# Join factors of the first dilated pair sent through DRAM instead of repeated and turned on chip

## The chip, the cores and the metric

The kernel runs on one core of a Trainium2 chip. The metric is the device time of one execution in microseconds (us); it is given as the median of three runs. The core has five engines that run side by side and meet by semaphores: TensorE (matmuls and transposes), VectorE, ScalarE, GpSimd and SyncE. SyncE's queue issues nearly all transfers of this kernel; 16 DMA engines carry them out. In the profile TensorE is called PE (its weight loads PEld), VectorE DVE, ScalarE ACT, GpSimd POOL and SyncE SP.

## The reference

A decoder trunk of two layers on 1024 tokens of width 1024, in float32. Each layer does

```python
h = rmsnorm(x, norm1[l])
qa, ka, va, qb, kb, vb, gate_pre = split(h @ w_in[l])
o_a = dilated_mixture(qa, ka, va)           # 12 heads of 64, three groups of 4
o_b = stick_breaking_attention(qb, kb, vb)  # 4 heads of 64
merged = g_a * (o_a @ w_br[l, :256]) + g_b * (o_b @ w_br[l, 256:])
x = x + merged @ w_o[l]
x = x + ffn(rmsnorm(x, norm2[l]))
```

The dilated mixture has three groups with dilation 1, 4 and 16. Each group gives an output `o` and a log-sum `lse` for each token and head, and the groups are mixed by

```python
alpha = softmax(stack(lses), axis=0)
o = sum(alpha[..., None] * stack(outs), axis=0)
```

So for every token and head there is one factor per group. A factor multiplies all 64 channels of its head at that token. This document is about how the factors get from where they are computed to where they multiply.

## The kernel before

**Layout.** Activations lie with channels on the 128 partitions and tokens along the free axis. The four mixture heads go in two pairs: pair 0 is heads 0 and 1, pair 1 heads 2 and 3. A pair's output fills 128 partitions: 64 channels of head 0 of the pair, then 64 of head 1. Group 1 (dilation 1) is computed by `near_item`, into the tile `on`. Groups 2 and 3 (dilation 4 and 16) are computed together by `far_item`, into the tile `ot`: eight items per pair (two heads, four residues `r` of the token modulo 4), named T00 to T07 for pair 0 and T10 to T17 for pair 1. So the mixture becomes a join of two parts, near and far.

**One far item.** `score` (L892) makes scores on TensorE (L646, L647, tile `z`), takes the row minimum of the negated scores on VectorE (L916) and the exponential with its row sum on ScalarE (L917, tile `p1`). `turn` (L921) transposes the result on TensorE (L924 to L926) into a PSUM bank with tag `t`, and splits it in a high and a low part (`parts`, L649): a cast on ScalarE (L141, `p1h`) and a subtraction on VectorE (L148, `p1l`). `apply` (L929) multiplies by the values (L934, L936). The last of these folds the result into `ot` (L661, L662) and, after the last item of a pair, calls `join`.

**Statistics and factors.** Minimum and sum of the far pass lie with tokens on partitions (tile `st1`). Those of the near pass come by way of DRAM (`dn`, `near_stats`, L948) in the same layout. `factors` (L952), called at the end of the score of the pair's last item, computes two factors (near and far) for each of 2 heads x 8 blocks of 128 tokens, in ten small instructions: tile `f`, 128 tokens x 2 x 16. A join needs them with channels on partitions, each repeated 64 times. So four ScalarE copies (L974) repeat each factor along the free axis into two tiles `fx` (tag `p4`, four buffers that the far items' `p1` also use), and `half_of` in `join` (L977) transposes them: eight 128x128 TensorE transposes (L988) per half of the tokens, into two PSUM banks, one with tag `t` and one with tag `o`. Then VectorE multiplies and adds in three instructions per half (L991 to L993), reading the factors from PSUM.

**Dense work and its order.** While the attention items run, projections of the layer run in between them, cut in shares of six 128x512 matmuls (class `Dense`, L222; L1017 to L1019). `attend` (L369) walks through the items and calls `dense.advance` between their steps; for far items it adds 0.58 of a share per step. `dense.at(n, f)` calls `f` when `n` more shares have been issued. `join` places its halves at 2 and at 4 (`JOIN`) shares. The order on TensorE is exactly the program's (a manual schedule). On the other engines a planner orders the instructions at build time, by priority (program order, or 200 ahead with `high_priority(offset=AHEAD)`) and by when it believes their inputs are ready; the order is then fixed, and each engine works through its queue in turn, waiting where an input is not there. `LAST["dve"]` holds the last split of a turn; a dependency without a semaphore on it keeps an instruction behind that split in VectorE's queue.

**Who reads the join.** The joined `on` is read by `in_two("a")` in `mixer` (L1353) after all items, when it is split into `oh_a`, `ol_a` for the branch projections. The tile `ot` has one buffer, used by pair 0, then by pair 1. The second pair's join is the last work before the branch projections.

Of the kernel before, what the change touches and what calls it, by code (L numbers as in the profile page):

```python
# [7 lines left out]
F32 = mybir.dt.float32  # L8
# [4 lines left out]
ALU = mybir.AluOpType  # L13
# [3 lines left out]
P = 128  # L17
T = 1024
D = 1024
KD = D // P  # L20
HF = 512
# [12 lines left out]
PT = 6  # L34
# [5 lines left out]
NO_SYNC = mybir.DependencyInfo(mybir.DependencyClass.NoSync, mybir.DependencyReason.DATA)  # L40
# [11 lines left out]
X_AT = (3, 5, 7, 9)  # L52
AHEAD = 200
JOIN = 4


def f32(ap):
# [4 lines left out]
def trunk_kernel(ctx, tc, x, norm1, w_in, b_gate, w_br, w_o, norm2, w_up, conv_w, conv_b, w_down, norm_f, out, depth=None, probe=None):  # L62
    nc = tc.nc
    act, dve, pe, pool = nc.scalar, nc.vector, nc.tensor, nc.gpsimd
# [21 lines left out]
    LAST = {}  # L86
# [34 lines left out]
    sq = [dr.tile([2, 2, 64, T], F32, name=f"sq{i}") for i in range(4)]  # L121
    sv = [dr.tile([P, n, KD, P], F32, name=f"sv{n}") for n in (4, 2, 2)]
    dn = [dr.tile([4, T], F32, name=f"dn{i}") for i in range(2)]

    def bank(tag, name):
        return ps.tile([P, 512], F32, tag=tag, name=name)
# [434 lines left out]
    R = {}  # L561
# [83 lines left out]
    def scores(o, qt, ql, k):  # L645
        pe.matmul(o, qt, k, start=True, stop=False, skip_group_check=True)  # L646
        pe.matmul(o, ql, k, start=False, stop=True, skip_group_check=True)  # L647

    def parts(src, n, name):  # L649

        hi, lo = small(name + "h", F32R), small(name + "l", F32R)
        with tc.high_priority(offset=AHEAD):
            split(hi[:, :n], lo[:, :n], src[:, :n], "is")
        return hi, lo
# [228 lines left out]
    def far_item(dense, pr, s, r, share):  # L883
        i = 8 * pr + 4 * s + r
        slot = 2 * pr + s
        if s == 0 and r == 0:
            R["st1", pr] = sb.tile([P, 2, 2, 2, 4], F32, tag="st1", bufs=2, name="st1")
            R["ot", pr] = None
        st = R["st1", pr]
        shared = {}  # L890

        def score():  # L892
            if r == 0:
                bias = share["bias"] = sb.tile([P, 2, 256], F32, tag="bias", name="bias1")
                dve.tensor_scalar(bias[:, 0, :], base0, 4.0 * SLOPES[4 + slot], None, ALU.mult)
                dve.tensor_scalar(bias[:, 1, :], base2, 4.0 * SLOPES[8 + slot], None, ALU.mult)
            bias = share["bias"]
            pt = shared["p"] = sb.tile([P, T], F32, tag="p4", bufs=4, name="p1")
            z0, z1 = bank("s", "z10"), bank("s", "z11")
            t = R["kq", i % 2]  # L900
            for g in range(2):
                scores(z0[:, P * g : P * g + P], t[:, g, 1, 0:P], t[:, g, 2, 0:P], t[:, g, 0, 0:P])
            for g in range(2):
                scores(z1[:, 256 * g : 256 * g + 256], t[:, g, 1, P:256], t[:, g, 2, P:256], t[:, g, 0, :])
            dense.scored = i + 1
            if (s, r) == (1, 0):
                near_stats(pr)
            for n in range(2):
                flat = pt[:, 256:768] if n else pt[:, 0:256]
                if n:  # L910
                    zz, pp, bb = z1, flat, bias.rearrange("p g c -> p (g c)")
                else:
                    zz, pp, bb = z0[:, 0:256].rearrange("p (g c) -> p g c", g=2), flat.rearrange("p (g c) -> p g c", g=2), bias[:, :, P:256]
                nm = st[:, 0, s, n, r : r + 1]
                with tc.high_priority(offset=AHEAD):
                    LAST["red"] = dve.tensor_tensor_reduce(pp, zz, bb, 1.0, 3e38, ALU.add, ALU.min, nm).ins.name  # L916
                    act.activation(flat, flat, AF.Exp, bias=nm, scale=-1.0, accum_out=st[:, 1, s, n, r : r + 1])  # L917
            if (s, r) == (1, 3):
                factors(pr)

        def turn(g):  # L921
            pt = shared["p"]
            tp = bank("t", "t1")
            pe.transpose(tp[:, 0:P], pt[:, P * g : P * g + P], ident)  # L924
            pe.transpose(tp[:, P : 2 * P], pt[:, 256 + 256 * g : 384 + 256 * g], ident)
            pe.transpose(tp[:, 2 * P : 3 * P], pt[:, 384 + 256 * g : 512 + 256 * g], ident)  # L926
            shared[g] = parts(tp, 384, "p1")

        def apply(g):  # L929
            if r % 2 == 0 and g == 0:  # L930
                share["o"] = bank("o", "o1")
            o, oc, vt = share["o"], 256 * (r % 2), R["v", i][:, g]
            for p in (0, 1):
                pe.matmul(o[:, oc : oc + 256], vt[:, 0:P], shared[g][p][:, 0:256], start=(r % 2 == 0 and g == 0 and p == 0), stop=False, skip_group_check=True)  # L934
# [12 lines left out]

    def near_stats(pr):  # L948
        sn = R["sn", pr] = sb.tile([P, 2, 2, 2, 4], F32, tag="sn", bufs=1, name="sn")
        nc.sync.dma_start(sn.rearrange("j a s n r -> j (a s) n r"), tok_view(dn[pr]))  # L950

    def factors(pr):  # L952

        sn, st = R["sn", pr], R["st1", pr]
        nat, far_ = (t.rearrange("j a s n r -> j a (s n r)") for t in (sn, st))
        w = sb.tile([P, 6, 16], F32, tag="sw", bufs=1, name="sw")
        f = R["f", pr] = sb.tile([P, 2, 2, 2, 4], F32, tag="sf", bufs=1, name="sf")
        ff = f.rearrange("j a s n r -> j a (s n r)")
        dve.tensor_tensor(w[:, 0, :], nat[:, 0, :], far_[:, 0, :], ALU.min)
        dve.tensor_tensor(w[:, 1, :], w[:, 0, :], nat[:, 0, :], ALU.subtract)  # L960
        dve.tensor_tensor(w[:, 2, :], w[:, 0, :], far_[:, 0, :], ALU.subtract)
        act.activation(w[:, 1:3, :], w[:, 1:3, :], AF.Exp)
        dve.tensor_tensor(w[:, 3, :], w[:, 1, :], nat[:, 1, :], ALU.mult)
        dve.tensor_tensor(w[:, 4, :], w[:, 2, :], far_[:, 1, :], ALU.mult)
        dve.tensor_tensor(w[:, 3, :], w[:, 3, :], w[:, 4, :], ALU.add)
        dve.reciprocal(w[:, 5, :], w[:, 3, :])
        dve.tensor_tensor(ff[:, 0, :], w[:, 1, :], w[:, 5, :], ALU.mult)
        dve.tensor_tensor(ff[:, 1, :], w[:, 2, :], w[:, 5, :], ALU.mult)

        R["fx", pr] = []  # L970
        for a in range(2):
            fx = sb.tile([P, 2, 4, 2, 64], F32, tag="p4", bufs=4, name="fx")
            for s in range(2):
                act.copy(fx[:, :, :, s, :], f[:, a, s, :, :].unsqueeze(3).to_broadcast([P, 2, 4, 64]))  # L974
            R["fx", pr].append(fx.rearrange("p n r s c -> p n r (s c)"))

    def join(dense, pr):  # L977

        fx, on, ot = R["fx", pr], R["on"], R["ot", pr]
        mine = on[:, pr, :].rearrange("p (n j r) -> p n r j", n=2, r=4)  # L980
        other = ot.rearrange("p (r n j) -> p n r j", r=4, n=2)

        def half_of(n):
            spread = []
            for a in range(2):
                o = bank("to"[a], "j_ps")
                for r in range(4):
                    pe.transpose(o[:, r * P : (r + 1) * P], fx[a][:, n, r, :], ident)  # L988
                spread.append(o.rearrange("p (r j) -> p r j", r=4))
            t = small("jn").rearrange("p (r j) -> p r j", r=4)  # L990
            dve.tensor_tensor(t, other[:, n], spread[1], ALU.mult)  # L991
            dve.tensor_tensor(mine[:, n], mine[:, n], spread[0], ALU.mult)
            dve.tensor_tensor(mine[:, n], mine[:, n], t, ALU.add)  # L993

        dense.at(2, lambda: half_of(0))
        dense.at(JOIN, lambda: half_of(1))

# [1174 lines left out]
```

## Time and profile before

| | |
|---|---|
| median of three runs | 2615.91 us (2615.09 to 2616.14) |
| the profiled execution | 2618.04 us |
| its span, from first to last instruction | 2616.1 us |
| TensorE busy | 2606.0 us |
| VectorE busy | 2089.5 us |
| ScalarE busy | 1357.6 us |
| GpSimd busy | 102.2 us |
| DMA queue of SP | 465.90 MB, 55.3% of 16 engines |

Times in rows of the trace are microseconds from the start of the span. A row of a time list has the start, the duration, the engine, the line, the operation, output and inputs, and in brackets how long the engine stood idle before and what ended that. A row of the chain of waits has start, duration, engine, tile and line; "issue" in it is time that the profile ascribes to nothing. Groups give minimum, median and maximum of the duration in nanoseconds, or busy time and mean. The shown duration of a matmul is longer than the interval between two of them, since they are pipelined; the interval between starts is what one costs.

### The profile page before, as it was taken

To read this page: it belongs to the slowest core of one execution; us is meant where nothing else is said; L and a number is where in the kernel's file an instruction comes from. 1 tells how busy PE (TensorE), PEld (TensorE's weight loads), DVE (VectorE), ACT (ScalarE), POOL (GpSimd) and SP (SyncE) were. 2 spreads that over 40 slices of the span, in tenths; PEclk is the share of its full clock that TensorE was granted. 3 is DMA by queue.
4 is the path that set the end of the run, shared out by engine and by line. 5 is a ranking of instruction groups with operands and counts; after the bars stand their busy time and mean duration, and the time that the engine had idled before them with its cause. 6 is when DMAs were issued, how large, how long until landed. Compare 5 with 4: busy or idle time off the path is not lost.

```text
span 2616.1 us, 36210 instructions
## 1 busy us (share of the span) xinstructions
PE 2606.0 (100%) x12736; PEld 2185.2 (84%) x12736; DVE 2089.5 (80%) x3484; ACT 1357.6 (52%) x2533; POOL 102.2 (4%) x135
## 2 busy tenths in 40 slices
PE   9999999999999999999999999999999999999999
PEld 8888888888888888888888888888888888888888
DVE  7877777795988888897677788777869888889965
ACT  6555666574554555422445555666645555544225
POOL 3000000020000000000000000000300000000000
PEclk9999999999999999999999999999999999999999
DMA  7434578873344444688344436787633344447962
GB/s 254 151 120 132 161 207 217 214 247 93 93 145 153 145 164 142 234 326 317 145 145 147 125 128 180 203 231 210 207 99 119 125 161 146 150 164 260 347 238 111
DMA packets 400418, 468.22 MB, mean 179 GB/s; under 512 B 24308, under 2 KB 315500, under 8 KB 398444
## 3 DMA queue, kind: packets, MB, share of 16 engines
q1 hardware_dynamic: 400220, 465.90, 55.3%
q8 instruction: 101, 1.65, 0.3%
q14 instruction: 81, 0.66, 0.1%
q10 hardware_dynamic: 16, 0.00, 0.0%
HBM read 303.23 MB, written 162.59 MB: 178 GB/s over the span
## 4 chain that ended last, share of the span: by engine, by line
PE 96%; DVE 1%; DMA 1%; ACT 1%; issue 1%; SPq 0%; POOL 0%; DVEq 0%; ACTq 0%
PE u_a L1019 6%; PE u_a L1018 6%; PE u_a L1017 6%; PE d_ps L1780 5%; PE d_ps L1781 5%; PE d_ps L1782 5%; PE i_a L1017 5%; PE i_a L1019 5%; PE i_a L1018 5%; PE u_c L1017 3%; PE u_c L1019 3%; PE u_c L1018 3%; PE i_c L1017 3%; PE i_c L1019 3%; PE i_c L1018 3%; PE o_ps L183 2%
## 5 line engine op out<-in xcount | busy, mean ns | idle before, releaser
L141 ACT CAST w_hi<-up_a 128x512 fp32r<-128x512 f32 x280 | 173.9, 622 | 276.5 <-DVE up_a L1634 120.5
L148 DVE TENSOR_TENSOR w_lo<-up_a,w_hi 128x512 fp32r<-128x512 f32 x280 | 189.3, 688 | 83.6 <-ACT w_hi L141 83.6
L141 ACT CAST w_hi<-in_a 128x512 fp32r<-128x512 f32 x252 | 156.2, 622 | 162.9 <-PE i_c L1018 38.0
L148 DVE TENSOR_TENSOR w_lo<-in_a,w_hi 128x512 fp32r<-128x512 f32 x252 | 172.7, 687 | 75.8 <-ACT w_hi L141 67.0
L1788 DVE TENSOR_TENSOR x<-x,d_ps 128x512 f32<-128x512 f32 (+1 forms) x228 | 153.4, 674 | 65.0 <-PE d_ps L1782 61.6
L1780 PE MATMUL d_ps<-gd_in,w_hi 128*128 128x512 f32 (+1 forms) x340 | 130.0, 382 | 0.0
L1782 PE MATMUL d_ps<-gd_in,w_lo 128*128 128x512 f32 (+1 forms) x340 | 129.8, 382 | 0.0
L1781 PE MATMUL d_ps<-gd_in,w_hi 128*128 128x512 f32 (+1 forms) x340 | 129.7, 382 | 0.0
L1019 PE MATMUL u_a<-hh,w_lo 128*128 128x512 f32 x320 | 124.5, 389 | 0.0
L1018 PE MATMUL u_a<-hl,w_hi 128*128 128x512 f32 x320 | 124.5, 389 | 0.0
L1017 PE MATMUL u_a<-hh,w_hi 128*128 128x512 f32 x320 | 124.5, 389 | 0.0
L1017 PE MATMUL u_a<-t_hi,w_hi 128*128 128x512 f32 x320 | 124.5, 389 | 0.0
L1019 PE MATMUL u_a<-t_hi,w_lo 128*128 128x512 f32 x320 | 124.5, 389 | 0.0
L1018 PE MATMUL u_a<-t_lo,w_hi 128*128 128x512 f32 x320 | 124.5, 389 | 0.0
L1017 PE MATMUL i_a<-hh,w_hi 128*128 128x512 f32 x288 | 119.2, 414 | 0.0
L1017 PE MATMUL i_a<-t_hi,w_hi 128*128 128x512 f32 x288 | 118.3, 411 | 0.0
L1780 PE MATMUL d_ps<-gd_in,wd 128*128 128x512 f32 (+1 forms) x292 | 113.9, 390 | 0.0
L1019 PE MATMUL i_a<-hh,w_lo 128*128 128x512 f32 x288 | 113.2, 393 | 0.0
L1019 PE MATMUL i_a<-t_hi,w_lo 128*128 128x512 f32 x288 | 113.0, 393 | 0.0
L1018 PE MATMUL i_a<-t_lo,w_hi 128*128 128x512 f32 x288 | 112.9, 392 | 0.0
L1018 PE MATMUL i_a<-hl,w_hi 128*128 128x512 f32 x288 | 112.8, 392 | 0.0
L1782 PE MATMUL d_ps<-gd_in,wd 128*128 128x512 f32 (+1 forms) x292 | 112.8, 386 | 0.0
(380 smaller groups left out, 7834.9 us busy)
## 6 DMA issues: line engine op xcount, KB each, us to landing
gd<-g SPq DMA_DIRECT2D x154, 512.0 KB, 3.3
gd_in<-gd SPq DMA_DIRECT2D x154, 512.0 KB, 5.9
up_a<-in_w_up_dram SPq DMA_DIRECT2D x80, 512.0 KB, 5.2
in_a<-in_w_in_dram SPq DMA_DIRECT2D x72, 512.0 KB, 5.3
wd_raw<-in_w_down_dram SPq DMA_DIRECT2D x22, 1024.0 KB, 11.2
gin<-gs SPq DMA_DIRECT2D x32, 512.0 KB, 3.8
w_raw<-in_w_o_dram SPq DMA_DIRECT2D x64, 256.0 KB, 2.9
gs<-u SPq DMA_DIRECT2D x48, 256.0 KB, 3.2
```

The source lines that it names most:

```text
L141: one = act.copy(hi, src)
L148: two = dve.tensor_tensor(lo, src, f32(hi), ALU.subtract)
L183: pe.matmul(o, lh, rl, start=False, stop=False, skip_group_check=share)
L1017: pe.matmul(o, w[0][:, c], rh, start=(first and i == 0), stop=False, skip_group_check=True)
L1018: pe.matmul(o, w[0][:, c], rl, start=False, stop=False, skip_group_check=True)
L1019: pe.matmul(o, w[1][:, c], rh, start=False, stop=(last and i == 3), skip_group_check=True)
L1780: pe.matmul(o[:, sub], wh[:, c], gh[:, sub], start=(i == 0 and k in (0, 4, 5)), stop=False, skip_group_check=True)
L1781: pe.matmul(o[:, sub], wh[:, c], gl[:, sub], start=False, stop=False, skip_group_check=True)
L1782: pe.matmul(o[:, sub], wl[:, c], gh[:, sub], start=False, stop=(i == m - 1), skip_group_check=True)
L1788: dve.tensor_tensor(x, x, o[:, sub], ALU.add)
```

## The change

For the first pair only (`pr == 0`), in both layers:

- `factors` writes the far factors in the order in which the tile `ot` has its tokens (residue before half), in two small VectorE instructions instead of one. The four ScalarE copies are not made.
- Four dense shares later (`SEND`), the 32 rows of factors are transposed once on TensorE (a 128x32 tile to 32x128), copied to SBUF by ScalarE, and written to a new DRAM tile `fd` (4 rows of 1024 tokens) by a transfer issued from GpSimd. Four more GpSimd-issued transfers read each row back, repeated over 64 partitions, into two tiles `fx` of 128 x 1024 (the same tag and size as the old ones).
- The join's halves are placed 3 and 5 shares after `join` instead of 2 and 4. They have no transposes: VectorE multiplies `ot` in place by the far factors, `on` by the near ones, and adds. Both multiplications are kept behind the last split of a turn.

The second pair's factors and join are as they were.

```diff
 JOIN = 4
+SEND = 4
...
+    fd = dr.tile([4, T], F32, name="fd")
...
             if (s, r) == (1, 3):
-                factors(pr)
+                factors(dense, pr)
...
-    def factors(pr):
+    def factors(dense, pr):
...
         dve.tensor_tensor(ff[:, 0, :], w[:, 1, :], w[:, 5, :], ALU.mult)
-        dve.tensor_tensor(ff[:, 1, :], w[:, 2, :], w[:, 5, :], ALU.mult)
+        if pr:
+            dve.tensor_tensor(ff[:, 1, :], w[:, 2, :], w[:, 5, :], ALU.mult)
+        else:
+            one, two = (w[:, k, :].rearrange("j (s n r) -> j s n r", s=2, n=2) for k in (2, 5))
+            for x in range(2):
+                dve.tensor_tensor(fr[:, 16 + 8 * x : 24 + 8 * x].rearrange("j (r n) -> j n r", n=2), one[:, x], two[:, x], ALU.mult)
+
+        if pr == 0:
+            R["fx", pr] = [sb.tile([P, T], F32, tag="p4", bufs=4, name="fx") for _ in range(2)]
+
+        def send():
+            tp = bank("t", "f_t")
+            pe.transpose(tp[0:32, 0:P], fr, ident)
+            row = sb.tile([32, P], F32, tag="pt", bufs=PT, name="f_r")
+            with tc.high_priority(offset=AHEAD):
+                act.copy(row, tp[0:32, 0:P])
+            nc.gpsimd.dma_start(fd.rearrange("c (k p) -> (c k) p", p=P), row)
+            for a in range(2):
+                for x in range(2):
+                    nc.gpsimd.dma_start(R["fx", pr][a][64 * x : 64 * x + 64, :], fd[2 * a + x : 2 * a + x + 1, :].to_broadcast([64, T]))
+
+        if pr == 0:
+            dense.at(SEND, send)
+            return
...
     def join(dense, pr):
...
+        def half_sent(n):
+            first, second = R["fx", pr]
+            mine, far = on[:, pr, n * HF : (n + 1) * HF], ot.rearrange("p (r n j) -> p n r j", r=4, n=2)[:, n]
+            mine = mine.rearrange("p (j r) -> p r j", r=4)
+            one = dve.tensor_tensor(far, far, second.rearrange("p (r n j) -> p n r j", r=4, n=2)[:, n], ALU.mult)
+            two = dve.tensor_tensor(mine, mine, first[:, n * HF : (n + 1) * HF].rearrange("p (r j) -> p r j", r=4), ALU.mult)
+            dve.tensor_tensor(mine, mine, far, ALU.add)
+            for x in (one, two):
+                tc.add_manual_dep(x.ins, LAST["dve"], NO_SYNC, reason="in turn")
+
+        if pr == 0:
+            dense.at(JOIN - 1, lambda: half_sent(0))
+            dense.at(JOIN + 1, lambda: half_sent(1))
+            return
```

More of the change, by code (lines that the diff above doesn't have):

```diff
@@ L958, in factors @@
         ff = f.rearrange("j a s n r -> j a (s n r)")
+        fr = f.rearrange("j a s n r -> j (a s n r)")
         dve.tensor_tensor(w[:, 0, :], nat[:, 0, :], far_[:, 0, :], ALU.min)
@@ L977, in join @@
     def join(dense, pr):
-        fx, on, ot = R["fx", pr], R["on"], R["ot", pr]
+        on, ot = R["on"], R["ot", pr]
+        def half_sent(n):
[11 more added lines that the diff above has]
+            return
+        fx = R["fx", pr]
         mine = on[:, pr, :].rearrange("p (n j r) -> p n r j", n=2, r=4)
```

## The prediction

> **What bounds the kernel.** I read the page's first part, then the chain of waits, then the time order of the stretch in which the first pair is joined.
>
> ```profile
> span 2616.1 us, 36210 instructions
> PE 2606.0 (100%) x12736; PEld 2185.2 (84%) x12736; DVE 2089.5 (80%) x3484; ACT 1357.6 (52%) x2533; POOL 102.2 (4%) x135
> PE 96%; DVE 1%; DMA 1%; ACT 1%; issue 1%; SPq 0%; POOL 0%; DVEq 0%; ACTq 0%
> ```
>
> TensorE carries 96% of the chain that ends last. So an instruction taken from TensorE is worth its interval, if nothing else is then late, and work taken from ScalarE or VectorE is worth something only where TensorE waits for it. The chain near the first layer's first join shows both kinds:
>
> ```profile
> 470.78 0.57 ACT fx L974
> ...
> 471.82 1.13 ACT fx L974 x2
> 472.95 0.53 ACT w_hi L141
> 473.51 0.69 DVE w_lo L148
> 474.20 0.60 DVE p L916
> ...
> 475.66 0.37 ACT p1h L141
> ...
> 476.05 0.57 DVE p1l L148
> ...
> 476.67 0.39 PE o L934
> ...
> 485.33 0.87 PE j_ps L988 x8
> ...
> 490.70 0.87 PE j_ps L988 x8
> ```
>
> The four copies that repeat the factors (L974) hold ScalarE from 470.78 to 472.95, 2.17 us; a weight cast, a split and a softmax step queue behind them, and TensorE's matmul of L934 comes late at 476.67. The same chain stands in layer 1. The waits of the two stretches, 460 to 510 and 1750 to 1800, have one wait of TensorE each, with the same row:
>
> ```profile
> PEld o L934 <- DVE p1l L148: 0.3, 1, 0.3
> ```
>
> **The change, step by step.** *Transposes removed.* Two groups of eight per first pair and layer (L988). TensorE in order of time, layer 0 (a fence for each stretch):
>
> ```profile
> 485.17 1.03 PE L988 MATMUL j_ps<-ident,fx 128*128 128x128 f32 x8
> 485.96 0.30 PE L646 MATMUL z<-t_kq 128*128 128x128 f32 x1
> ```
> ```profile
> 490.54 1.03 PE L988 MATMUL j_ps<-ident,fx 128*128 128x128 f32 x8
> 491.41 0.27 PE L924 MATMUL t<-ident,p 128*128 128x128 f32 x1
> ```
>
> ```profile
> 1776.78 1.04 PE L988 MATMUL j_ps<-ident,fx 128*128 128x128 f32 x8
> 1777.57 0.30 PE L646 MATMUL z<-t_kq 128*128 128x128 f32 x1
> ```
>
> The durations are latencies of pipelined instructions; the price is from start to next start: 485.96 - 485.17 = 0.79 and 491.41 - 490.54 = 0.87, together 1.66 us a layer. Layer 1's first group, the third fence, takes 0.79 too; I count its two like those of layer 0: 3.32 us in all.
>
> *One transpose added* per layer (32 columns), in the fourth dense share after the factors. One of eight costs 0.79 / 8 = 0.10 us, so 0.20 is lost in all. Its bank has the tag of the turns; the turn before last has been split long before, so I see no wait for a bank there.
>
> *Four copies removed from ScalarE, one small copy added.* The nearest rows are the copies themselves and the small copy of the near pass (same shape):
>
> ```profile
> 471.22 0.69 DVE L1145 TENSOR_TENSOR in_a<-in_a 128x512 f32<-128x512 f32 x1
> 476.67 0.19 PEld L934 LDWEIGHTS o<-p1l,slots 128*128 128x128 f32 x1 [0.32 <-DVE p1l L148]
> ```
> ```profile
> L844 ACT COPY st_r<-st_t x4: 254/254/254, 373.0 to 1712.2; 32x128 f32<-32x128 f32 x4
> ...
> DMA to landing us min/median/max: 2.9/3.4/3.9
> ```
>
> Off the path but for the wait above. Without L974 the weight cast can start when its source is ready, 471.22 + 0.69 = 471.9 instead of 472.9, some 1.0 us earlier, and the 0.25 us copy falls after it; 1.0 - 0.25 covers the wait of 0.32 us, so I count the wait as gone: 0.64 us in two layers. Next late there would be nothing that the rows show: TensorE has no other wait in either stretch.
>
> *VectorE.* One operation on 16 columns becomes two on 8: one instruction more a layer, dearer than nothing and cheaper than the 0.55 us of a 384-column split (row below), where VectorE is busy 7.46 of 10 us (stretch 470 to 480, below): 0. The join's three operations keep their sizes; two that read PSUM now read SBUF. The rows give no difference between such sources:
>
> ```profile
> L992 DVE TENSOR_TENSOR on<-on,j_ps x8: 1056/1088/1096, 485.8 to 1833.6; 128x512 f32<-128x512 f32 x8
> L991 DVE TENSOR_TENSOR jn<-ot,j_ps x8: 671/678/701, 486.8 to 1833.0; 128x512 f32<-128x512 f32 x8
> L993 DVE TENSOR_TENSOR on<-on,jn x8: 1059/1088/1130, 487.8 to 1835.1; 128x512 f32<-128x512 f32 x8
> ```
>
> L992 reads PSUM, L993 only SBUF, both 1088 ns. So nothing, but both halves move one share later, and their cover is VectorE's idle time there (below).
>
> *Transfers and the new wait.* Five on GpSimd's queue: 16 KB to DRAM, a wait until it has landed, then four of 256 KB, each to 64 partitions. GpSimd has no other work between 470 and 500 (the stretches further below give it 0.00), so nothing is queued behind the wait. SP's queue gets nothing. No row shows a transfer issued by GpSimd. Nearest are those issued by SP: the near pass's statistics (the same 32x128 row, landed after 3.4 us, quoted above), and 256 KB loads to 64 partitions, three of which were issued in 2.47 us:
>
> ```profile
> 341.42 2.47 SPq L693 DMA_DIRECT2D slots<-sq  x3
> ```
> ```profile
> kv<-sk SPq DMA_DIRECT2D x16, 256.0 KB, 4.6
> slots<-sq SPq DMA_DIRECT2D x24, 256.0 KB, 5.5
> ```
> ```profile
> L1399 POOL TENSOR_TENSOR hl<-mrg,hh 128x512 fp32r<-128x512 f32 x32 | 43.6, 1370 | 302.9 <-ACT hh L1398 302.9
> ```
>
> When must they be there? The fourth share after the factors ends where the first turn of the last far item begins (473.75); the first sent half may start after the split of the turn that stands before its share (its manual order), which is this one on VectorE:
>
> ```profile
> 473.75 0.27 PE L924 MATMUL t<-ident,p 128*128 128x128 f32 x1
> ...
> 486.97 0.28 PE L924 MATMUL t<-ident,p 128*128 128x128 f32 x1
> ```
> ```profile
> 489.36 0.55 DVE L148 TENSOR_TENSOR p1l<-t,p1h 128x384 fp32r<-128x384 f32 x1
> 491.30 0.69 DVE L148 TENSOR_TENSOR w_lo<-in_a,w_hi 128x512 fp32r<-128x512 f32 x1 [1.40 <-ACT w_hi L141]
> ```
>
> 489.36 + 0.55 = 489.9 is its end now, with the 2.85 us of the old first half (1.09 + 0.68 + 1.09) ahead of it; without that half and with TensorE 0.79 + 0.32 - 0.10 = 1.0 us ahead I put it at about 487.5 (an estimate: its transposes are at 486.97, less 1.0, plus 0.4 for them, 0.5 for the cast, 0.55 for itself). The small row is in SBUF at 473.75 + 0.3 + up to 0.7 of waiting + 0.25 = 475.0. Cheap end: 475.0 + 3.4 = 478.4; issues of 2.47 / 3 = 0.82 us, the last issued 2.5 us after the first, landing 4.6 later: 485.5, 2 us early. Dear end with overlap: each issue takes as long as GpSimd's costliest group (1.37): 475.0 + 1.4 + 3.4 = 479.8, then 4 x 1.37 + 5.5: 490.8, or 3.3 us late. Below nothing they cannot go: an earlier landing gives nothing. I take the cheap end, since shape, size and partitions are those of its rows: 0.
>
> Where they are late, VectorE stands in its order, with the splits of weights and turns behind it, for which TensorE waits. Cover is the idle 1.40 us before 491.30. The dear end so costs 3.3 - 1.4 = 1.9 us a layer, 3.8 in all. The results have time: the joined pair is first read near 534.
>
> ```profile
> L141 ACT CAST oh_a<-on x8: 615/620/622, 534.1 to 1836.2; 128x512 fp32r<-128x512 f32 x8
> ```
>
> [...]
>
> *DMA load.* 1 MB more per layer onto engines that are half free when the pieces run:
>
> ```profile
> 470.00:480.00 10.00, 9.87 (x61) 8.50 (x61) 7.46 (x18) 6.29 (x14) 0.00 (x0) 1.00 1.02 252
> 480.00:490.00 10.00, 10.00 (x62) 8.77 (x61) 8.57 (x18) 5.76 (x14) 0.00 (x0) 1.00 0.58 145
> 490.00:500.00 10.00, 10.00 (x64) 8.83 (x63) 7.91 (x16) 6.12 (x15) 0.00 (x0) 1.00 0.63 153
> ...
> 540.00:560.00 20.00, 20.00 (x90) 16.55 (x89) 19.17 (x25) 12.09 (x20) 5.55 (x4) 1.00 0.90 307
> ```
>
> A row is the stretch, its length, busy time of TensorE, its weight loads, VectorE, ScalarE and GpSimd, the clock, the DMA share and GB/s. The share is 0.58 where the pieces run. The loads beside them bring the scores' and values' tiles for items ahead; from the last item's first turn at 473.75 to that of the next but one at 486.97 are 13.2 us, 6.6 an item, and a score's load is issued an item or more ahead, so it bears some us of delay: 0.
>
> *Buffers.* The two factor tiles hold two of four buffers some 3 us longer; scores need the other two only. The far result's buffer is wanted again when the second pair's first fold comes, behind the second half on VectorE anyway: 0.
>
> **Sum.** -3.32 + 0.20 - 0.64 + 0 = -3.8 us. Against the profiled execution's 2618.04 (span 2616.1 and 1.9 around it) that is 2614.2; it lies 2.1 above the median of the runs, 2615.91, to which the same difference gives 2612.1. That is 0.15%. About 0.2%, or 5.2 us, is what a measurement of this kernel can tell from no change.
>
> **Rivals.** *Slower: the four pieces come one behind another.* All four read rows of one 16 KB block in DRAM, 64 readers to a row, which no row of this profile shows, and GpSimd generates them. Four times 4.6 after 478.4 is 496.8, 9.3 us late; less 1.4, VectorE's stop costs TensorE 7.9 us a layer: -3.8 + 15.8 = +12.0, 2627.9. It decides against the change once the lateness passes 1.4 + 1.9 = 3.3 us a layer. For it: nothing shows such reads. Against: the three loads above overlap. [...] The trace's three loads in 2.47 us with 5.5 to landing speak against a full 4.6 for each.
>
> *Hidden only in part*: the dear end, 0.0, 2615.9, or anything between that and the forecast.
>
> *The wait on ScalarE stays*: the planner orders ScalarE and VectorE anew, and another operation stands where the copies stood. Then -3.1, 2612.8: only the transposes pay, and it stays within 0.2%.
>
> *Faster by more than 5.2 us.* VectorE loses the burst beside the second score, and ScalarE 1.9 us a layer; a better order after the join could give 0.7 us or more a layer. The waits list speaks against it: TensorE has no more idle time there to win; it would have to come from the branch stage, where VectorE is busy 19.17 of 20 us (last row above). Another 2.1 us in all gives 2610.0.
>
> **How the numbers follow.** Forecast with the ScalarE variant 0.62 (2610.7 to 2614.5), of which 0.05 passes -0.2%; hidden in part 0.10, all within 0.2%; pieces late by more than the cover 0.20, of which 0.02 stays within 0.2%; faster by order 0.08. So faster 0.13, same 0.57 + 0.10 + 0.02 = 0.69, slower 0.18. The range goes from 2609.5 to 2624: above it lies the upper part of the late case (0.12), below it 0.05. The likeliest case's own range is 2610.7 to 2614.5.
>
> **What would show it.** Right: no L988 group near 484 and 1775, one 32-column transpose near 473.8; no wait of L934 near 476; GpSimd's five transfers between 475 and 486, the last landed before the first half's multiply; VectorE's multiplies with no wait for a DMA; TensorE's time between the same matmuls, from the last far item's score to the second pair's join, shorter by about 1.9 us. Wrong: VectorE idle before the first sent half with a DMA as releaser, and a TensorE wait for a split just behind it; or a TensorE wait elsewhere in the far items that takes back the gain.

## The result, and the profile after

The changed kernel takes 2623.23 us (median of nine runs, 2620.29 to 2625.21); the kernel before, run beside it, takes 2615.40 (2615.01 to 2616.14). The ratio is 1.0027, with a 95% interval of 1.0017 to 1.0037: slower by 7.8 us, where 3.8 less were forecast. The time lies in the range given, but on the wrong side of the kernel before. The range reached so far up only for a rival whose mechanism did not come, as shown below, so this is luck. The profiled execution of the changed kernel took 2621.13 us. In the changed file most lines are 2 further down, those behind the new functions 42: L934 is now L936, L148 is L150, L1017 to L1019 are L1059 to L1061; the transpose of the factors is L983, their copy L986, the write to DRAM L987, the read-back L990, a sent half L1011 to L1013.

The head of the page after:

```profile
span 2619.4 us, 36184 instructions
PE 2603.4 (99%) x12706; PEld 2182.2 (83%) x12706; DVE 2092.1 (80%) x3486; ACT 1355.3 (52%) x2527; POOL 106.2 (4%) x145
```

TensorE is busy 2.6 us less than before (2606.0), in a span that is 3.3 longer. So the work was taken away, and something made TensorE stand.

*The saving came.* TensorE in order of time, where the factors are turned and where the wait of 0.32 us behind ScalarE's copies had been:

```profile
472.64 0.27 PE L983 MATMUL f_t<-ident,sf 128*32 128x128 f32 x1
472.74 0.27 PE L926 MATMUL t<-ident,p 128*128 128x128 f32 x1
...
475.37 0.28 PE L936 MATMUL o<-p1l,slots 128*128 128x256 f32 x1
```

The one transpose costs 472.74 - 472.64 = 0.10 us, and the multiplication at 475.37 waits for nothing (no bracket).

*The transfers are late.* GpSimd in order of time in both layers, then the times to landing of the two writes of 16 KB, then those of the eight read-backs of both layers:

```profile
474.49 0.67 POOL L987 DMA_DIRECT2D fd<-f_r  x1 [55.40 <-ACT f_r L986]
480.37 2.04 POOL L990 DMA_DIRECT2D fx<-fd  x4 [5.21 <-PE o L938]
```
```profile
1767.47 0.54 POOL L987 DMA_DIRECT2D fd<-f_r  x1 [55.38 <-ACT f_r L986]
1773.79 2.04 POOL L990 DMA_DIRECT2D fx<-fd  x4 [5.78 <-PE o L938]
```
```profile
DMA to landing us min/median/max: 5.3/5.5/5.8
```
```profile
DMA to landing us min/median/max: 6.0/7.5/8.9
```

The write lands 5.3 and 5.8 us after its issue, and to the issue of the first read-back pass 5.9 and 6.3 us. (The bracket names a TensorE instruction, whose shown ends, 480.32 and 1773.31, lie 0.05 and 0.48 us before these issues; the landing lies 0.6 and 0.5 before them, and with the row elsewhere and the later halves, below, the bracket in layer 0 names it. So I take the landing for what ended the wait.) The last of layer 0's four read-backs, issued about 481.9, lands 8.9 later, at 490.8. VectorE and TensorE behind it, in order of time:

```profile
485.84 0.56 DVE L150 TENSOR_TENSOR p1l<-t,p1h 128x384 fp32r<-128x384 f32 x1 [0.24 <-ACT p1h L143]
490.87 0.69 DVE L1011 TENSOR_TENSOR ot<-ot,fx 128x512 f32<-128x512 f32 x1 [4.47 <-DMA fx<-fd]
```
```profile
1783.40 0.69 DVE L1011 TENSOR_TENSOR ot<-ot,fx 128x512 f32<-128x512 f32 x1 [3.58 <-DMA fx<-fd]
```
```profile
494.64 0.38 PE L936 MATMUL o<-p1l,slots 128*128 128x256 f32 x1 [1.28 <-DVE p1l L150]
499.36 0.39 PE L936 MATMUL o<-p1l,slots 128*128 128x256 f32 x1 [2.32 <-DVE p1l L150]
```
```profile
1787.19 0.39 PE L936 MATMUL o<-p1l,slots 128*128 128x256 f32 x1 [0.84 <-DVE p1l L150]
1791.92 0.39 PE L936 MATMUL o<-p1l,slots 128*128 128x256 f32 x1 [2.31 <-DVE p1l L150]
```

VectorE stands 4.47 and 3.58 us with a DMA as releaser. Then both halves come almost back to back, as they do without any such stand too (see the run without transfers), and the splits of two turns come late. TensorE waits 3.60 us in layer 0 and 3.15 in layer 1.

*And the clock halves once.* After the second wait of layer 1 the same matmuls, which start 0.23 us apart at 1796.82 and 1797.05, start 0.42 apart at 1792.60 and 1793.02. Two stretches of 3.41 us (the stretch, its length, TensorE's busy time and instructions, granted clock, DMA share, GB/s):

```profile
1789.18:1792.59 3.41, 1.10 (x7) 1.00 0.18 67
1792.59:1796.00 3.41, 3.41 (x12) 0.50 0.15 58
```

TensorE was busy 1.10 of 3.41 us, and the next 3.41 us ran at clock 0.50, which loses 1.7 us of work. The trace of before has none between its first and last microseconds.

Together: -3.8 + 6.7 (waits) + 1.7 = +4.6 us. The two profiled executions differ by 3.1 (before's lay 2.6 above its median), the medians by 7.8. A second half clock, in layer 0, would make 6.3. The nine runs fall into four at 2620.3 to 2621.1 and five at 2623.2 to 2625.2, and the mean clock of all five is 0.998, that of three of the four 0.999, which fits one half clock or two, but the trace shows only one of the nine, so this is not shown. The last 1.5 us of the median stay without an account.

*The load.* Transfers issued from 480 to 492 us, with KB each and median us to landing, before and then after:

```profile
t_kq<-tk SPq DMA_DIRECT2D x2, 384.0 KB, 4.7
...
slots<-tv SPq DMA_DIRECT2D x2, 256.0 KB, 4.4
```
```profile
fx<-fd POOLq DMA_DIRECT2D x4, 256.0 KB, 7.9
t_kq<-tk SPq DMA_DIRECT2D x2, 384.0 KB, 7.9
...
slots<-tv SPq DMA_DIRECT2D x2, 256.0 KB, 7.7
```

SyncE's loads went from 4.4 and 4.7 to 7.7 and 7.9 us, about as long as GpSimd's read-backs of like size. In the same 12 us, the share of the 16 DMA engines that SyncE's transfers took before, and the share that the read-backs take after (packets, MB, share):

```profile
q1 hardware_dynamic: 1220, 1.97, 65.2%
```
```profile
q0 software_dynamic: 320, 1.05, 38.4%
```

Together they would fill the engines (1.04), and the share after is 0.94 to 1.07 in each 2 us from 480 to 492. This points to a queue that both share, the DMA engines, more than to GpSimd's own; the experiments test it.

### The profile page after: what moved, and what is told of

Its sections match the earlier page's. It is cut to its first block, busy times and chain, and to the rows that moved or that the text cites. A ratio compares the mean times of both kernels' runs of the same rounds, so it can differ in the third digit from the quotient of the medians.

```text
span 2619.4 us, 36184 instructions
## 1 busy us (share of the span) xinstructions
PE 2603.4 (99%) x12706; PEld 2182.2 (83%) x12706; DVE 2092.1 (80%) x3486; ACT 1355.3 (52%) x2527; POOL 106.2 (4%) x145
## 3 DMA queue, kind: packets, MB, share of 16 engines
q0 software_dynamic: 704, 2.13, 0.4%
## 4 chain that ended last, share of the span: by engine, by line
PE 98%; DVE 1%; ACT 0%; issue 0%; POOL 0%; DVEq 0%; POOLq 0%; ACTq 0%
PE u_a L1059 6%; PE u_a L1060 6%; PE u_a L1061 6%; PE d_ps L1822 5%; PE d_ps L1824 5%; PE d_ps L1823 5%; PE i_a L1059 5%; PE i_a L1061 5%; PE i_a L1060 5%; PE u_c L1059 3%; PE u_c L1060 3%; PE u_c L1061 3%; PE i_c L1059 3%; PE i_c L1061 2%; PE i_c L1060 2%; PE o_ps L184 2%
## 5 line engine op out<-in xcount | busy, mean ns | idle before, releaser
L150 DVE TENSOR_TENSOR w_lo<-up_a,w_hi 128x512 fp32r<-128x512 f32 x280 | 189.3, 688 | 83.7 <-ACT w_hi L143 83.7
L150 DVE TENSOR_TENSOR w_lo<-in_a,w_hi 128x512 fp32r<-128x512 f32 x252 | 172.7, 687 | 71.6 <-ACT w_hi L143 63.7
L1059 PE MATMUL u_a<-hh,w_hi 128*128 128x512 f32 x320 | 124.5, 389 | 0.0
L1061 PE MATMUL u_a<-hh,w_lo 128*128 128x512 f32 x320 | 124.5, 389 | 0.0
L1059 PE MATMUL u_a<-t_hi,w_hi 128*128 128x512 f32 x320 | 124.5, 389 | 0.0
L1061 PE MATMUL u_a<-t_hi,w_lo 128*128 128x512 f32 x320 | 124.5, 389 | 0.0
L1059 PE MATMUL i_a<-hh,w_hi 128*128 128x512 f32 x288 | 119.1, 414 | 0.0
L1059 PE MATMUL i_a<-t_hi,w_hi 128*128 128x512 f32 x288 | 118.5, 411 | 0.0
L1061 PE MATMUL i_a<-t_hi,w_lo 128*128 128x512 f32 x288 | 113.5, 394 | 0.0
L1061 PE MATMUL i_a<-hh,w_lo 128*128 128x512 f32 x288 | 113.1, 393 | 0.0
```

The lines of the kernel that those rows point to most:

```text
L150: two = dve.tensor_tensor(lo, src, f32(hi), ALU.subtract)
L1059: pe.matmul(o, w[0][:, c], rh, start=(first and i == 0), stop=False, skip_group_check=True)
L1061: pe.matmul(o, w[1][:, c], rh, start=False, stop=(last and i == 3), skip_group_check=True)
```

## The experiments

Theory W: the change saves 3.8 us, and all the loss is the late read-back. For the lateness: L (bytes on loaded DMA engines), G (GpSimd's issue), H (64 reads of one row). Rival R: something else in the change costs. Rival C: the added bytes hold other loads back. The kernel before ran beside all of these: its medians were 2616.36, 2616.59, 2616.49 and 2616.24 in four sessions. PE is TensorE, DVE is VectorE in the rows.

**Multiplies that do not read the transfers.**

```diff
-            one = dve.tensor_tensor(far, far, second...[:, n], ALU.mult)
-            two = dve.tensor_tensor(mine, mine, first[...]..., ALU.mult)
+            one = dve.tensor_tensor(far, far, ident.unsqueeze(1).to_broadcast([P, 4, P]), ALU.mult)
+            two = dve.tensor_tensor(mine, mine, ident.unsqueeze(1).to_broadcast([P, 4, P]), ALU.mult)
```

> The five transfers stay, but the join's multiplies of the first pair read a constant tile (the identity, each 128 columns again) in place of the factors read back, so the output is not the reference's. Theory (the transfers land late, VectorE stands for them and TensorE loses 3.6 and 3.1 us behind it): no DMA wait on VectorE, no wait of L936 near 494 and 499, and the time falls to the forecast's -3.8 us against the kernel before, about 2611.6. Rival (the loss comes from other loads, delayed by 1 MB more on the DMA engines, or from the new order of the engines): the transfers are as before, so the time stays at 2620 or above.

Measured: 2619.94 us, ratio 1.0014 (1.0005 to 1.0022). Still slower than before, which seemed to speak for R. The waits say otherwise (who waits for whom: us in total, times, longest):

```profile
DVE p L918 <- DMA fx<-fd: 3.6, 1, 3.6
```
```profile
PE o L936 <- ACT p1h L143: 3.3, 2, 1.7
```

The tiles of factors had no reader any more, so the next score's `p1` took such a buffer, and its row minimum (L918) waited for the same landing. The wait had only moved; with 3.7 us of TensorE's waits in all and two half clocks of 1.7, the account gives -3.8 + 3.7 + 3.4 = +3.3, and 3.6 was measured. The run did not separate W from R; the next one does.

**No transfers.** As above, and `fx`, the write and the four read-backs left out.

> All five transfers are left out and the four multiplies read the identity in SBUF, so the first pair's output is not the reference's; the transposes of 32 columns and the copy behind it stay. What I hold now (W): the change saves TensorE 3.8 us, and what it loses comes from the late read-back alone: VectorE's stand, TensorE's wait behind it, and the half clock of 3.4 us that the trace shows behind such a wait in the second layer. Then nothing is late here: no wait of TensorE over 0.5 us near 490 and 1785, the full clock throughout, and 3 to 4 us less than the kernel before. Rival R (something else of the change costs, such as the new order on VectorE or the stretch of the joins without TensorE's transposes): the time stays at or above the kernel before, with a wait of TensorE near the joins that has nothing to do with a DMA.

Measured: 2612.24 us, ratio 0.9985 (0.9976 to 0.9994). No wait of TensorE is listed in either layer's stretch of joins, and no half clock. 4.4 us less than before: this fits the saving of 3.8 (the interval of the ratio is 1.6 to 6.3 us), and R falls. VectorE in order of time, where the two halves begin:

```profile
485.93 0.56 DVE L150 TENSOR_TENSOR p1l<-t,p1h 128x384 fp32r<-128x384 f32 x1 [0.24 <-ACT p1h L143]
486.41 0.68 DVE L1003 TENSOR_TENSOR ot<-ot,ident 128x512 f32<-128x512 f32 x1
...
490.08 0.67 DVE L1003 TENSOR_TENSOR ot<-ot,ident 128x512 f32<-128x512 f32 x1
```

From 485.93 to beyond 494 no wait of VectorE is listed here. So the halves stand 3.67 us apart without any stand before them, as in the change (490.87 and 494.51, 3.64 apart).

**Transfers that run, with a late reader.** The first form added one column's read of both tiles at the end of the second half:

```diff
             dve.tensor_tensor(mine, mine, far, ALU.add)
+            if n:
+                dve.tensor_tensor(first[:, 0:1], first[:, 0:1], second[:, 0:1], ALU.mult)
```

> The transfers stay as they are, but the multiplies read the identity, so the first pair's output is not the reference's; the two tiles of factors are read once, one column of each, behind the second half, so that their buffers come free when they did. W: no wait at the first half, and a time within 1 us of the run without transfers (3 to 4 us under the kernel before). Rival C (the 1 MB of reads in a layer slows SyncE's loads of keys and values, and the pieces behind them come late): 2 to 5 us above the run without transfers, with VectorE or TensorE waiting on tiles that SyncE loads or on what is made from them.

Measured: 2626.16 us (five runs), ratio 1.0037 (1.0023 to 1.0050). The planner put this read, which depended on nothing but the transfer, ahead of the first half:

```profile
DVE fx L1015 <- DMA fx<-fd: 12.4, 2, 6.4
```
```profile
PE o L936 <- ACT p1h L143: 6.8, 2, 3.5
```

So it priced a longer wait: TensorE 7.2 us, two half clocks 3.4, less 3.8: +6.8 by the account, +9.6 measured. The second form ties the read to the half's last sum:

```diff
+                end = mine[:, 3, P - 1 : P]
+                dve.tensor_tensor(second[:, 0:1], second[:, 0:1], end, ALU.mult)
```

> The late-touch run again with the one-column reads of the factors tied to the last sum of the second half, since VectorE took them ahead of the first half there; the multiplies read the identity, so the first pair's output is not the reference's. W: all transfers run and nothing waits for them: within 1 us of the run without transfers (2612.2 us). C (the 1 MB of reads in a layer delays SyncE's loads of keys and values, or the buffers it fills, and what is made from them): 2 us or more above that run, with a wait of TensorE or VectorE for such a tile.

Measured: 2613.77 us, ratio 0.9988 (0.9979 to 0.9997). The read-backs were as late as ever, but nobody waited (times to landing; TensorE's longest wait in layer 1):

```profile
DMA to landing us min/median/max: 5.5/6.9/9.9
```
```profile
PE o L936 <- DVE fx L1016: 0.2, 1, 0.2
```

With both halves still back to back, the loss is gone but for 1.5 us against the run without transfers, of which 0.4 are TensorE's waits. The intervals of the two runs overlap, so even these 1.5 are not clear of the noise. So the wait and what follows from it are the cause, and C is worth little, by these medians about 1 us.

**Why late: half the bytes.**

```diff
-  nc.gpsimd.dma_start(R["fx", pr][a][64 * x : 64 * x + 64, :], fd[2 * a + x : 2 * a + x + 1, :].to_broadcast([64, T]))
+  nc.gpsimd.dma_start(R["fx", pr][a][64 * x : 64 * x + 64, 0:HF], fd[2 * a + x : 2 * a + x + 1, 0:HF].to_broadcast([64, HF]))
```

> The four read-backs fetch only the first 512 of each row's 1,024 factors, and both halves multiply by those, so the first pair's output is not the reference's. Issues, places and descriptors' rows stay, the bytes are halved. L (lateness is the queue of bytes on the loaded DMA engines: 1 MB at the 230 GB/s of these stretches is 4.6 us): the landings fall by about 2 us, from 6.0 to 8.9 us down to 4 to 6.5; the first multiply waits 2.5 and 1.5 us instead of 4.5 and 3.6, TensorE's four waits sum to 2 to 3 us instead of 6.7, and the time is 2614 to 2618. G (the issues by GpSimd and what stands ahead of the bytes set it): landings stay at 6 us and more, and the time stays at 2620 to 2625.

Measured: 2615.99 us, ratio 0.9998 (0.9989 to 1.0007), with landings and TensorE's waits of

```profile
DMA to landing us min/median/max: 5.1/5.4/7.5
```
```profile
PE o L936 <- DVE p1l L150: 2.9, 2, 1.9
```

VectorE waits 2.5 and 0.7 us instead of 4.5 and 3.6. The median landing falls by 2.1 us, as L expected, at unchanged issues. The longest, 7.5, is above the 6.5 that L gave: the bytes are a part of the lateness, and what makes the rest is open.

**Why late: other rows.** The read-backs fetch 64 different rows:

```diff
-  nc.gpsimd.dma_start(R["fx", pr][a][...], fd[2 * a + x : 2 * a + x + 1, :].to_broadcast([64, T]))
+  nc.gpsimd.dma_start(R["fx", pr][a][...], xs[0][64 * x : 64 * x + 64, 2 * a : 2 * a + 2, :].rearrange("p a b -> p (a b)"))
```

> Each read-back fetches 64 different rows of 4 KB of a tensor in DRAM instead of one row 64 times, and the multiplies use these, so the first pair's output is not the reference's; the 16-KB write stays, but the read-backs do not wait for it. H (64 reads of the same 4 KB come in turn from one place of the memory): measured from issue, the landings fall from 6.0 to 8.9 us to 5 us or less. L (bytes on loaded engines): from issue they stay at 6 to 9 us; since they can start up to 5 us earlier, the wait at the first multiply may go all the same, so this is read from the landings and not from the time.

```profile
DMA to landing us min/median/max: 7.1/8.4/9.3
```

From issue they are no faster than one row read 64 times (median 7.5), where H expected 5 us or less, so H falls as far as this run goes: half of its read-backs run some 17 us earlier, at 463. The kernel's time, 2621.03 us (ratio 1.0018, 1.0009 to 1.0027), answers nothing here: its issues stand elsewhere, TensorE waits 4.1 us in other places, and some 4 us of it have no account.

**Who issues.** All five transfers from SyncE:

```diff
-            nc.gpsimd.dma_start(fd...., row)
+            nc.sync.dma_start(fd...., row)
...
-                    nc.gpsimd.dma_start(R["fx", pr][a]...)
+                    nc.sync.dma_start(R["fx", pr][a]...)
```

> The five transfers are issued from SP's queue in place of GpSimd's. If the lateness is the price of transfers that GpSimd generates, the row lands in 3.4 and the pieces in 4.6 us as SP's others do, VectorE hardly waits, and the time is 2612 to 2615. If it is the load on the 16 DMA engines, the pieces take 7 to 9 us as now, the time is not under 2620, and since SP's queue stands for the row's landing, the scores' loads behind it come later as well: up to 2630.

Measured: 2617.39 us, ratio 1.0004 (0.9996 to 1.0013), VectorE's waits for the read-back summing to 3.4 us instead of 8.1. SyncE's queue in layer 0:

```profile
474.61 0.38 SPq L987 DMA_DIRECT2D fd<-f_r  x1
...
478.87 0.48 SPq L990 DMA_DIRECT2D fx<-fd  x1
```

From write to read-back 4.3 us instead of GpSimd's 5.9. But in layer 1 it is 6.5 us, against 6.3:

```profile
1765.10 0.39 SPq L987 DMA_DIRECT2D fd<-f_r  x1
...
1771.57 0.48 SPq L990 DMA_DIRECT2D fx<-fd  x1
```

So this run does not show a share of G. SyncE's loads queued behind that wait stood for 2.9 us. What that costs was not separated, nor whether the transfers are quicker because no other load is issued meanwhile.

**Another place.** The send one share earlier, or the halves one share later:

```diff
-SEND = 4
+SEND = 3
```

> The factors are sent one dense share sooner (SEND 3 for 4), so 2.3 us earlier. Theory of lateness: VectorE's waits of 4.5 and 3.6 us fall to about 2.2 and 1.3, TensorE's of 3.6 and 3.1 us to about 1.3 and 0.8, total about 4.6 us less than the changed kernel: 2616 to 2619. Rival (other loads or order): no change, 2620 to 2625. If the landing takes longer because it now meets a fuller stretch of the DMA engines, the waits fall by less than 2.3.

```diff
-            dense.at(JOIN - 1, lambda: half_sent(0))
-            dense.at(JOIN + 1, lambda: half_sent(1))
+            dense.at(JOIN, lambda: half_sent(0))
+            dense.at(JOIN + 2, lambda: half_sent(1))
```

> Both halves of the join one share later (4 and 6 for 3 and 5). Theory of lateness: like sending one share sooner, VectorE's waits fall by about 2.2 us each, time 2616 to 2619. Rival: no change. A second rival: the second half now stands next to the first fold of the second pair, so what is won at the first half is lost there, and the time stays above 2619.

Measured: 2618.42 us (ratio 1.0006, 0.9998 to 1.0015) with the earlier send, 2617.78 (1.0008, 0.9999 to 1.0017) with the later halves. With the later halves VectorE still waits 7.4 us for the read-back, but TensorE only 2.7, since the halves stand further apart. With the earlier send no multiply waits, but VectorE has another wait, in both layers:

```profile
477.13 0.56 DVE L150 TENSOR_TENSOR p1l<-t,p1h 128x384 fp32r<-128x384 f32 x1 [2.15 <-DMA fd<-f_r]
```
```profile
1768.45 0.56 DVE L150 TENSOR_TENSOR p1l<-t,p1h 128x384 fp32r<-128x384 f32 x1 [3.14 <-DMA fd<-f_r]
```

The small row `f_r` lies in a buffer of a tag with six, which the split wants while the 16-KB write is still reading it.

> The send stands one piece earlier (SEND 3) and both halves one piece later (pieces 4 and 6). W: either alone left a remainder (1.8 us of TensorE's waits with the earlier send, 2.7 us with the later halves), together the first multiply finds its tile landed; what stays is the wait of a split for the buffer that the 16-KB write still reads (3.1 us of VectorE at most with the earlier send). So 1 to 3 us under the kernel before, and the clock full or halved once. R: no better than either alone, at or above the kernel before.

Both together: 2616.73 us, ratio 1.0002 (0.9993 to 1.0010). The split still waits for the write (3.8 us at most), and the profiled execution had two half clocks. W's 1 to 3 us under before did not come; the next change takes that wait away.

**The row elsewhere.** The row is put into the second tile of factors, which the read-back fills only after the write.

```diff
-            row = sb.tile([32, P], F32, tag="pt", bufs=PT, name="f_r")
+            row = R["fx", pr][1][0:32, 0:P]
```

> The send stands one piece earlier (SEND 3) and the row that is written to DRAM lies in the second tile of factors, which the read-back fills only after that write, so no split waits for its buffer. W, with that second wait: with the earlier send alone the multiplies waited for nothing and what stayed were VectorE's waits of a split for the 16-KB write (2.2 and 3.1 us) with 1.2 and 0.6 us of TensorE and one half clock behind them; without these the saving of 3.8 us is whole: 2611.5 to 2613.5, no DMA among VectorE's waits near 480 and 1775, the clock full throughout. R (the earlier place only moves the wait to another tile): a wait of TensorE of 1 us or more is left, and the time is 2615 or more.

Measured with SEND 3 and the halves as in the change: 2617.83 us, ratio 1.0002 (0.9993 to 1.0012). W's 2611.5 to 2613.5 was wrong here. The wait for the write is gone, and the multiplies wait again:

```profile
DVE ot L1011 <- DMA fx<-fd: 4.3, 2, 2.5
```
```profile
PE o L936 <- DVE p1l L150: 4.0, 2, 2.1
```

So with the earlier send alone the multiplies had found their tiles. That VectorE was held up there by the split, 2.15 us in layer 0, does not by itself explain it. The landings of that run's read-backs, both layers:

```profile
DMA to landing us min/median/max: 3.7/5.1/6.8
```

Its last read-back of layer 0 was issued at 479.1 and so had landed by 486.0. The first multiply came at 488.8; 2.15 us earlier, at 486.6, the tile would still have been there. With the row in the tile of factors the write took 6.2 us to the next issue, not 5.2, and a read-back up to 9.4 us to land. Why, no run separates.

> As the run with the row in the tile of factors and SEND 3, and both halves one piece later besides (pieces 4 and 6). W: the transfers had landed anyway, so the later halves bring nothing: within 0.7 us of that run. R (landings vary from run to run and the multiplies wait in some runs): 1 us or more faster than that run and less spread.

With the later halves as well: 2614.44 us (2612.49 to 2617.18), ratio 0.9993 (0.9984 to 1.0001); TensorE's waits behind a split come to 0.2 us. The later halves bring 3.4 us by the medians, which the rival (landings that vary) expected and W did not; the two intervals overlap. GpSimd in layer 0, landings of writes and read-backs of both layers, and the first multiply in layer 1:

```profile
472.24 0.67 POOL L987 DMA_DIRECT2D fd<-fx  x1 [52.87 <-ACT fx L986]
477.66 2.05 POOL L990 DMA_DIRECT2D fx<-fd  x4 [4.75 <-DMA fd<-fx]
```
```profile
DMA to landing us min/median/max: 3.9/6.0/9.7
```
```profile
1778.80 0.69 DVE L1011 TENSOR_TENSOR ot<-ot,fx 128x512 f32<-128x512 f32 x1 [3.05 <-DMA fx<-fd]
```

A stop of VectorE of 3.05 us costs TensorE almost nothing where the second half does not follow at once.

> As the last version (SEND 3, the row in the tile of factors), with the halves at pieces 5 and 7. W (the rest of the loss is the wait for landings that vary, with a half clock behind each long one): the first multiply waits for nothing in either layer, no half clock, and 2612 to 2613.5, with less spread than 4.7 us. Rival P (what is left comes from the place of the multiplies among VectorE's splits, not from the landings): no faster than with pieces 4 and 6 (2614.4), with TensorE waits behind a split and no DMA among VectorE's releasers.

One share later still: 2615.26 us, ratio 0.9996 (0.9987 to 1.0006), no multiply waits, but TensorE waits 1.7 us behind a split without any DMA. Rival P: that place has its own cost.

> As the version with SEND 3, the row in the tile of factors and pieces 4 and 6, but all five transfers are issued by SyncE. G (GpSimd's issue or its way of making descriptors adds to the lateness): at least 1 us faster than with GpSimd (2614.4), no DMA wait on VectorE. L (only the queue of bytes): within 1 us, or slower where SyncE's wait for the 16-KB write (2.9 us in the earlier run from SyncE) holds its loads of keys and values back.

SEND 3, row in the tile of factors, pieces 4 and 6, all from SyncE: **2612.36 us** (2611.68 to 2613.16), ratio 0.9985 (0.9977 to 0.9994), the one version that multiplies by the true factors and beats the kernel before beyond the interval. SyncE's queue in layer 0, then the last read-back and the first multiply in layer 1:

```profile
471.68 0.32 SPq L987 DMA_DIRECT2D fd<-fx  x1
...
475.79 1.75 SPq L990 DMA_DIRECT2D fx<-fd  x3
```
```profile
1769.79 0.60 SPq L990 DMA_DIRECT2D fx<-fd  x1
```
```profile
1777.15 0.69 DVE L1011 TENSOR_TENSOR ot<-ot,fx 128x512 f32<-128x512 f32 x1 [1.65 <-DMA fx<-fd]
```

At the same place the write's 4.1 us to the next issue stand against GpSimd's 5.4, and in layer 1 5.4 against 6.3. The trace resolves only two of the ten landings here, so their spread can't be compared; the multiply of layer 1 still waited for a read-back until 7.4 us after the last one's issue (1777.15 - 1769.79), against GpSimd's 9.7 at most. The runs spread over 1.5 us instead of 4.7. TensorE has no wait in either stretch. That is G's side of the expectation, except for one DMA wait that cost nothing. But SyncE, standing for the write, also issued other loads later: one of `slots` at 474.77 and one at 481.15 with GpSimd, none from 470 to 486.9 here. So whether the gain comes from who issues or from the loads that start later stays open.

## Why the prediction was wrong

- *Transposes removed, one added, two waits on ScalarE gone* (-3.32 + 0.20 - 0.64 = -3.8): right. 0.10 us for the transpose, no wait near 475, and 4.4 and 2.7 us under before in the two runs whose multiplies read the identity and in which next to nothing waited.
- *Transfers and the new wait*: this step failed, at "I take the cheap end, since shape, size and partitions are those of its rows: 0". The row was in SBUF at 474.2, earlier than the 475.0 put down. But the write took 5.3 us to land and 5.9 to the next issue, not 3.4, and the last read-back 8.9 to land, not 4.6. It landed at 490.8, just where the dear end had it, by luck, since the terms were others: issues of 0.5 us instead of 1.37, landings longer than the 3.4 and 5.5. The rows with the same shape were not from the place where the transfers run; the load there was in the quoted row of 470 to 480, share 1.02. A row of the trace before gave a warning: the 16 KB of the near pass's statistics read back (`sn<-dn`) took 6.0 and 6.8 us in the two cases that the trace resolves. It is issued by SyncE and has another shape, but the one of 6.0 us was issued at 1767.9, 0.4 us from where the change issues its row in layer 1.
- *When they must be there*: estimated at 487.5; VectorE was ready at 486.4 (485.84 + 0.56). Lateness was 4.5 and 3.6 us, not 3.3.
- *Cover of 1.40 us*: too large. Of 4.47 and 3.58 us, TensorE lost 3.60 and 3.15, so 0.4 to 0.9 was covered. The idle 1.40 us was read from the order before; in the changed order it does not exist, as the run without transfers shows: no wait of VectorE stands in it from the first half to beyond the second.
- *DMA load: 0*: wrong at its root. The engines called half free were 65% taken from 480 to 492, and the read-backs add 38%. Loads there went from 4.4 us to 7.7. It cost little through SyncE's loads (theory C, about 1 us), but the read-backs ran on the same 16 engines, whose share was 0.94 to 1.07; with half the bytes their median landing fell by 2.1 us.
- *Buffers: 0*: nothing was lost in the change as made, but two buffers decided variants: the row's and the tiles of factors.
- *Rivals*: "decides against the change once the lateness passes 3.3 us a layer" has the wrong cover in it: with 0.4 to 0.9 us the border is 2.3 to 2.8 us, and lower with a half clock; 4.5 and 3.6 passed either. The mechanism given, pieces one behind another at 4.6 us each, is not what the trace shows: four landed within 10.4 us of the first issue. From issue to landing a piece took 6.0 to 8.9 us, the row 5.3 and 5.8.
- Nowhere priced: the half clock behind a wait, 1.7 us each, one in the profiled execution.

## What to carry to other kernels

Take a transfer's time to landing from rows of the stretch in which it will run, and add the bytes of the change to that stretch first; here 65% and 38% filled the 16 engines (0.94 to 1.07), and rows of the same shape or size from elsewhere, 3.4 and 4.6 us, said little of the 5.3 and 5.8, and 6.0 to 8.9, that came. Take idle time that is to cover a delay from the order after the change, not from the one before. Where the engine that waits also feeds TensorE, keep the pieces of work behind the wait apart (8.1 us of VectorE's waits cost TensorE 6.7 here, 7.4 cost it 2.7 with the halves further apart), and give the source row of a transfer a buffer that nobody wants soon (a split stood up to 3.8 us for it). A wait of TensorE may cost twice its length: 1.7 us of half clock came behind one of 1.7.

## What the runs showed of the hardware

The half clock came behind a TensorE wait of 1.7 us, and not always. In stretches of 3.41 us, the length of the half clock in the trace of the change, counted from a trace's first full clock, over the eleven profiles that have a TensorE wait of 0.5 us or more at the joins: of thirteen stretches with TensorE busy for less than 1.9 us, ten were followed by one stretch at 0.50; of those busy longer, none. The busy time alone does not decide: 1.52 us were not followed by a half clock, 1.88 in another run were. One pair, from the run whose multiplies read the identity, where no wait at the joins was over 1.7 us:

```profile
488.91:492.33 3.42, 1.57 (x8) 1.00 1.05 226
492.33:495.74 3.41, 3.41 (x16) 0.50 0.08 23
```

In each of the ten the half clock filled one stretch so counted, at 0.50 over the whole of it. TensorE did not have to stand through the stretch ahead: here it was busy for 1.57 of 3.42 us. In layer 0 of the change the waits of 3.60 us fell into two stretches, busy for 2.13 and 1.52 us, and no half clock followed. So it may be that the same waits cost 1.7 us more or not by where the border of a stretch falls, and that this is one reason for the spread of these variants; this is my guess, and no run separates it.
